# A mixture-of-experts block: experts placed by load, 12 in pairs of 64 slots and 52 in fours of 32 slots

## The chip, the cores and the metric

One core of a Trainium2 chip runs the whole block in one launch. The metric is the device time of that core in microseconds (us). Three runs of the kernel before took 1903.79, 1905.90 and 1906.02 us; their median is 1905.9 us.

## The reference

A transformer block on 512 tokens of width 1024 in float32: a differential attention, a state-space branch, their merge, and then a mixture of 64 experts. Only the last part is changed:

```python
# h2: 512 x 1024 tokens after the norm; each token goes to 2 of the 64 experts (1024 assignments)
g_sel  = argmax(h2 @ w_gr + b_gr)                 # one of 8 groups of 8 experts
top_i  = top_k((h2 @ w_er + b_er)[g_sel], 2)      # two experts inside the group
weight = softmax(group)[g_sel] * softmax(top_v)
# for each expert e, on its tokens x:
y = (silu(x @ w_gate[e]) * (x @ w_up[e])) @ w_down[e]    # 1024 -> 512 -> 1024
out[token] += weight * y
return rms_norm(x + out) * final_norm_w
```

How many tokens an expert gets is known only once the router has run on the chip. The reference has no limit on it.

## The kernel before

Ahead of the experts come the projections, attention, the state-space branch and the router, ordered by a planner (`Flow`), which places jobs by costs written in the code. The experts' part is written out by hand, in program order for each engine.

**Work of a pair.** The loop at L1702 takes 32 pairs of experts in the order of their numbers. An expert has 64 slots; the 128 slots of a pair fill the 128 columns of TensorE's array as two column tiles of 64. For a pair, `gate_up` (L1627) runs over 8 pieces k of the contraction: for each expert of the pair a gate matmul and an up matmul of 128x64 stationary activations against 128x512 float32 weights (each recorded as two matmul instructions, so 64 in all for a pair). `combine` (L1685) adds the outputs of the pair before to the tokens by 16 matmuls, which DVE adds to `x`. `hidden_t` (L1644) turns the hidden activations, `slots` (L1612) builds the matrix that scatters slots back to tokens, `down` (L1653) runs 4 pieces of the down projection (32 recorded matmuls), `weighted` (L1665) scales and splits the result. Every second pair, `onehot` (L1404) makes the 0/1 matrix that picks tokens for the next four experts by comparing their ranks in the table `rk1` with 1 to 64, and `gather` (L1601) applies it by 64 matmuls to give the activations `xt` of the next two pairs.

**Weights.** The expert weights are 64 x 6 MB, loaded by SP's DMA queue alone. A tile of 1 MB holds piece k of both experts of a pair; `tiles` (L1195) lists 12 of them per pair in the order of use. `issue` (L1203) starts one load; every fifteenth tile goes to two staging buffers in two halves. There is room for 15 tiles. `free` and `fill` (L1548, L1551), called by `done` (L1690) after every piece k, issue the next load as soon as its buffer is free. The first 15 tiles are loaded ahead of the experts' part, while the router still runs. The last tile is loaded in four parts (L1561).

**Experts with more than 64 tokens.** `overflow_tables` (L1565), run by DVE in the first pair, lists further rounds of 64 slots for them. Behind the pairs, a loop at L1741 runs as often as the table says, with weights whose address comes from a register. The first number of the table is read into a register of every engine (L1739). The last combination, the final norm and the stores follow (L1772 on). `keep_warm` (L298) issues matmuls whose result is not used.

Of the kernel before, what the change touches and what calls it, by code (L numbers as in the profile page):

```python
# [24 lines left out]
class Flow:  # L25
    """Orders the work of the engines: every job names an engine, its length and the jobs it needs."""
# [92 lines left out]
def block_kernel(ctx: ExitStack, tc: tile.TileContext, I, out):  # L119
# [158 lines left out]
    G.iota(iota1, pattern=[[1, 64]], base=1, channel_multiplier=0, allow_small_or_imprecise_dtypes=True)  # L278
    rev8 = cst([128, 8], "rev8")
# [864 lines left out]
    class Part:  # L1144
        """A row of the merged activations, cut into halves of the tokens; part 0 or 1 of the split."""
# [49 lines left out]
    tiles = []  # L1195
    for p in range(32):
        tiles += [("gu", p, k) for k in range(8)] + [("dn", p, k) for k in range(4)]
# [3 lines left out]
    NE = NB - 6 + NX  # L1201

    def issue():  # L1203
        n = nxt["i"]
        nxt["i"] += 1
        kind, p, k = tiles[n]
        src = I[kind][p, :, k]
        if n % NE == XS:
            t = [stage(), stage()]
        else:  # L1210
            b = (mt("ewx", [128, 2048], "ew") if n % NE == 0 else big("ew")).rearrange("p (e n) -> p e n", e=2)
            t = [b[:, 0], b[:, 1]]
        wt[kind, p, k] = t
        if n + 1 == len(tiles):
            return
        if n % NE == XS:
# [169 lines left out]
    def rtabs():  # L1386
        R["ovi"] = mt(None, [128, 64], "ovi", I32)
        R["base"] = mt(None, [128, 16], "base")
# [15 lines left out]
    def onehot(p, cs=range(NCH)):  # L1404
        if 0 in cs:
            R["P", p] = mt("P", [128, NCH, 4, E], "P", F32R)
        for c in cs:
            V.tensor_tensor(R["P", p][:, c], rk1[:, c, 4 * p:4 * p + 4].unsqueeze(2).to_broadcast([128, 4, E]),  # L1408
                            iota1[:, None, :].to_broadcast([128, 4, E]), op=OP.is_equal)
        return R["P", p].rearrange("p c e s -> p c (e s)")  # L1410
# [12 lines left out]
    def route(cl, prev):  # L1423
# [46 lines left out]
        def rk():  # L1470
            V.scalar_tensor_tensor(rk1[:, cs].rearrange("p c e -> p (c e)"), R["rps"][:, cl[0] * E:cl[-1] * E + E], 1.0,
                                   R["ab"][:, cs].rearrange("p c g e -> p (c g e)"), op0=OP.add, op1=OP.mult)
            R["P0"] = onehot(0, cl)
# [77 lines left out]
    def fill():  # L1551
# [3 lines left out]
        if nxt["i"] == len(tiles) and not nxt["end"]:  # L1555
            nxt["end"] = True
            kind, p, k = tiles[-1]
            for i in range(2):
                h = slice(i * 512, i * 512 + 512)
                for e in range(2):  # L1560
                    nc.sync.dma_start(wt[kind, p, k][e][:, h], I[kind][p, :, k, e, h])  # L1561

    fill()

    def overflow_tables():  # L1565
        ex = mt("y", [128, 1024], "ex")
        ext, pe, pf = (ex[:, i * E:i * E + E] for i in range(3))
        io, ef = ex[:, 256:272], ex[:, 320:384]
        V.tensor_scalar(ext, R["cnt"], 64.0, None, op0=OP.is_gt)
        for m in range(2, 8):  # L1570
            V.scalar_tensor_tensor(ext, R["cnt"], 64.0 * m, ext, op0=OP.is_gt, op1=OP.add)
        a, b = ext, pe
        for sft in (1, 2, 4, 8, 16, 32):
# [3 lines left out]
        V.tensor_scalar(io, iota1[:, :16], -1.0, None, op0=OP.add)  # L1577
        le = mt("y", [128, 16, E], "le")
        V.tensor_tensor(le, a[:, None, :].to_broadcast([128, 16, E]), io.unsqueeze(2).to_broadcast([128, 16, E]),
                        op=OP.is_le)  # L1580
        V.memset(ef, 0.0)
        V.tensor_copy(ef[:, 0:1], a[:, E - 1:E])
        V.tensor_reduce(ef[:, 1:17], le, axis=AX.X, op=OP.add)
        V.tensor_scalar(ef[:, 1:17], ef[:, 1:17], float(E - 1), None, op0=OP.min)
        V.tensor_scalar(ef[:, 17:33], ef[:, 1:17], 0.5, -0.25, op0=OP.mult, op1=OP.add)
        V.tensor_scalar(ef[:, 17:33], ef[:, 17:33], 12582912.0, None, op0=OP.add)
        V.tensor_scalar(ef[:, 17:33], ef[:, 17:33], 12582912.0, None, op0=OP.subtract)
        V.scalar_tensor_tensor(ef[:, 33:49], ef[:, 17:33], -2.0, ef[:, 1:17], op0=OP.mult, op1=OP.add)
        V.tensor_copy(R["ovi"], ef)
        V.tensor_tensor(le, le, ext[:, None, :].to_broadcast([128, 16, E]), op=OP.mult)  # L1590
        V.tensor_reduce(R["base"], le, axis=AX.X, op=OP.add)
        V.tensor_tensor(R["base"], iota1[:, :16], R["base"], op=OP.subtract)
        V.tensor_scalar(R["base"], R["base"], 64.0, None, op0=OP.mult)

# [17 lines left out]
    def slots(P, n, wcols):  # L1612
        w = 64 * n
        ps = side()
        for c in range(NCH):
            T.transpose(ps[:w, c * 128:c * 128 + 128], P[:, c].bitcast(F32), ident)
        pt = mt("pt", [128, 512], "pt", F32R)[:w]
        V.tensor_copy(pt, ps[:w])
        ws = side()
        for c in range(NCH):  # L1620
            T.matmul(ws[:w, :n], lhsT=P[:, c].bitcast(F32), rhs=wcols(c), start=(c == 0), stop=(c == 3))
        sl = pools["mp"].tile([128, 1], F32, name="sl", bufs=2)[:w]
        for e in range(n):
            V.tensor_scalar(sl[64 * e:64 * e + 64], ws[64 * e:64 * e + 64, e:e + 1], 0.5, None, op0=OP.mult)
        return pt, sl

    def gate_up(xt, n, gu, done, pre=lambda q: None):  # L1627
        w = 64 * n
# [9 lines left out]
        hh = mt("ta", [128, 512], "hh")[:w]  # L1638
        A.activation(hh, pg[:w], AF.Tanh, scale=0.5)  # L1639
        V.scalar_tensor_tensor(hh, hh, 1.0, pg[:w], op0=OP.add, op1=OP.mult)  # L1640
        V.tensor_tensor(hh, hh, pu[:w], op=OP.mult)
        return hh

    def hidden_t(hh, n):  # L1644
        w = 64 * n
        ps = side()
        for k in range(4):
            T.transpose(ps[:, k * w:k * w + w], hh[:, k * 128:k * 128 + 128], ident[:w, :w])
        ht = mt("ta", [128, 4, 128], "hT")[:, :, :w]
        A.activation(ht, ps[:, :4 * w].rearrange("p (k n) -> p k n", k=4), AF.Copy)  # L1650
        return ht

    def down(ht, n, dn, done):  # L1653
        w = 64 * n
        ps = [side(), side()]
        for k in range(4):
            for i in range(2):
                for e in range(n):
                    es_ = slice(64 * e, 64 * e + 64)
                    T.matmul(ps[i][es_], lhsT=ht[:, k, es_], rhs=dn(k)[e][:, i * 512:i * 512 + 512],  # L1660
                             start=(k == 0), stop=(k == 3), tile_position=(0, 64 * e))
# [3 lines left out]
    def weighted(ps, n, sl, yt=None):  # L1665
        w = 64 * n
        yh, yl = (yt or [mt("y", [128, 2, 512], n_, F32R) for n_ in ("yh", "yl")])
        yh, yl = yh[:w], yl[:w]
# [226 lines left out]
```

## Time and profile before

| | |
|---|---|
| median of 3 runs | 1905.9 us |
| span of the profiled execution | 1903.0 us |
| TensorE matmul busy | 1855.0 us (97%), 9551 matmuls |
| DVE busy | 893.9 us (47%) |
| ScalarE busy | 463.5 us (24%) |
| GpSimd busy | 315.9 us (17%) |
| DMA traffic | 475.24 MB, mean 250 GB/s |

The execution of the profile has a span of 1903.0 us, from its first to its last instruction; the median of the runs is 2.9 us longer. All rows are of this execution. In the page's 40 slices each slice is 47.6 us; the digits are tenths of a slice in which an engine was busy. A row of stages gives the stretch, then busy time and number of instructions of PE (matmuls), PEld (weight loads into the array), DVE, ACT and POOL, then the granted clock of TensorE (1.00 is full), the mean busy share of the 16 DMA engines, and what they moved. Rows of the order in time give start, duration, engine, line, operation, output<-input, shapes and count.

### The profile page before, as it was taken

Reading aid. Unit: us, or ns where it says so; the run is one execution under the profiler, and the core shown is the slowest. Engines: PE = TensorE matmul, PEld = TensorE weight load, DVE = VectorE, ACT = ScalarE, POOL = GpSimd, SP = SyncE. Lnnn points to the kernel's source line nnn. Section 1 sums busy time; section 2 is a strip of 40 time slices with the busy share of each in tenths; the row PEclk is TensorE's granted clock in tenths of the full one; section 3 lists DMA queues with packets and bytes.
Section 4 is the critical chain, followed back from the end, with each engine's and each line's share of the span. In section 5 each row is a group of like instructions: output and inputs, shape, how many; then the busy total and the mean of one; then the engine's idle time right before and its main releaser. Section 6 shows DMA issues by size and latency. Waiting matters only on the chain. (4 is left out here: it accounts for less than half of the span.)

```text
span 1903.0 us, 24077 instructions
## 1 busy us (share of the span) xinstructions
PE 1855.0 (97%) x9551; PEld 1208.8 (64%) x9551; DVE 893.9 (47%) x1659; ACT 463.5 (24%) x913; POOL 315.9 (17%) x330
## 2 busy tenths in 40 slices
PE   8999999999999999998999999999999999999996
PEld 6877788878787787885554555455545554555453
DVE  7687832587886945444432323232323232323234
ACT  5355530344443422121111111011101110111012
POOL 5243321253544442111000000000000000000001
PEclk9999999999999999998999999999999999999998
DMA  5311123212222222467899999999999999999991
GB/s 163 100 56 46 45 80 98 78 56 89 68 67 77 78 78 89 149 239 286 349 421 393 397 392 420 394 395 393 421 395 395 398 418 393 399 395 405 406 396 71
DMA packets 81042, 475.24 MB, mean 250 GB/s; under 512 B 10145, under 2 KB 10529, under 8 KB 34977
## 3 DMA queue, kind: packets, MB, share of 16 engines
q1 hardware_dynamic: 80928, 473.70, 64.1%
q8 instruction: 76, 1.25, 0.3%
q14 instruction: 38, 0.30, 0.0%
HBM read 471.56 MB, written 2.10 MB: 249 GB/s over the span
## 5 line engine op out<-in xcount | busy, mean ns | idle before, releaser
L1635 PE MATMUL g<-ew,xt 128*64 128x512 f32 x1896 | 418.7, 594 | 0.0
L243 PE MATMUL g<-hH,w 128*128 128x512 f32 x1024 | 344.6, 401 | 0.0
L1635 PEld LDWEIGHTS g<-ew,xt 128*64 128x64 f32 x1896 | 169.1, 137 | 236.3 <-issue 231.0
L243 PEld LDWEIGHTS g<-hH,w 128*128 128x128 f32 x1024 | 192.4, 188 | 43.1 <-issue 5.3
L1660 PE MATMUL s<-ew,hT 128*64 128x512 f32 x968 | 216.0, 595 | 0.7 <-ACT hT L1650 0.7
L1640 DVE SCALAR_TENSOR_TENSOR hh<-hh,g 128x512 f32<-128x512 f32 x32 | 22.0, 688 | 411.6 <-ACT hh L1639 411.6
L243 PE MATMUL g<-hL,w 128*128 128x512 f32 x512 | 199.9, 390 | 0.0
L1796 POOL TENSOR_TENSOR fst<-fst 128x1 f32<-128x1 f32 x4 | 1.2, 301 | 1020.6 <-ACT fo L1789 1020.6
L203 DVE TENSOR_TENSOR w<-stg,w 128x1024 fp32r<-128x1024 f32 x108 | 140.9, 1313 | 55.7 <-ACT w L200 32.2
L1683 DVE TENSOR_TENSOR x<-x,s 128x512 f32<-128x512 f32 x256 | 155.8, 681 | 8.3 <-PE s L1678 8.3
L1660 PEld LDWEIGHTS s<-ew,hT 128*64 128x64 f32 x968 | 66.7, 137 | 121.3 <-issue 119.9
L1671 DVE SCALAR_TENSOR_TENSOR yl<-s,sl,yh 128x512 fp32r<-128x512 f32 x64 | 48.0, 751 | 182.3 <-ACT yh L1670 180.8
L1418 PE MATMUL s<-P,h2H 128*128 128x256 f32 x512 | 125.2, 286 | 2.4 <-DVE P L1408 2.4
L1677 PE MATMUL s<-yh,pt 128*128 128x512 f32 x256 | 113.5, 443 | 11.9 <-DVE x L1683 9.7
L1419 PE MATMUL s<-P,h2L 128*128 128x256 f32 x512 | 122.7, 282 | 0.0
L1639 ACT ACTIVATE hh<-g 128x512 f32<-128x512 f32 x32 | 19.2, 599 | 412.4 <-PE g L1635 412.4
L198 POOL TENSOR_SCALAR w<-stg 128x1024 fp32r<-128x1024 f32 x60 | 69.0, 1150 | 264.3 <-DMA stg<-in_wu_dram 178.3
L243 PEld LDWEIGHTS g<-hL,w 128*128 128x128 f32 x512 | 96.4, 188 | 16.9
L1418 PEld LDWEIGHTS s<-P,h2H 128*128 128x128 f32 x512 | 96.9, 189 | 10.1 <-issue 7.4
L1678 PE MATMUL s<-yl,pt 128*128 128x512 f32 x256 | 100.9, 394 | 0.0
L1670 ACT ACTIVATE yh<-s,sl 128x512 fp32r<-128x512 f32 x64 | 43.9, 687 | 231.8 <-PE s L1660 219.9
L1419 PEld LDWEIGHTS s<-P,h2L 128*128 128x128 f32 x512 | 97.0, 190 | 0.0
(312 smaller groups left out, 2666.1 us busy)
## 6 DMA issues: line engine op xcount, KB each, us to landing
ew<-in_gu_dram SPq DMA_DIRECT2D x237, 1024.0 KB, 11.0
ew<-in_dn_dram SPq DMA_DIRECT2D x120, 1024.0 KB, 14.6
stg<-in_wu_dram SPq DMA_DIRECT2D x120, 512.0 KB, 3.6
stg<-in_gu_dram SPq DMA_DIRECT2D x38, 512.0 KB, 9.9
stg<-in_dn_dram SPq DMA_DIRECT2D x14, 512.0 KB, 14.3
xT<-in_xT_dram SPq DMA_DIRECT2D x4, 512.0 KB, 5.7
x<-in_xn_dram SPq DMA_DIRECT2D x2, 1024.0 KB, 9.9
out_dram<-fo SPq DMA_DIRECT2D x8, 256.0 KB, 2.1
```

Of the source, the lines that this page charges most:

```text
L198: G.tensor_scalar(c["h"], c["st"], 1.0, 0.0, op0=OP.mult, op1=OP.add)
L203: (G if i % 10 == 9 else V).tensor_tensor(c["lo"], c["st"], c["h"].bitcast(F32), op=OP.subtract)
L243: T.matmul(cell[b], lhsT=x, rhs=y, start=first and i == 0, stop=last and i == 2)
L1418: T.matmul(o, lhsT=h2(h2H, c)[:, d], rhs=P[:, c], start=(c == 0), stop=False)
L1419: T.matmul(o, lhsT=h2(h2L, c)[:, d], rhs=P[:, c], start=False, stop=(c == NCH - 1))
L1635: T.matmul(o[es_], lhsT=xt[:, k, es_], rhs=gu(k)[e][:, i * 512:i * 512 + 512], start=(k == 0), stop=(k == 7), tile_position=(0, 64 * e))
L1660: T.matmul(ps[i][es_], lhsT=ht[:, k, es_], rhs=dn(k)[e][:, i * 512:i * 512 + 512], start=(k == 0), stop=(k == 3), tile_position=(0, 64 * e))
L1670: A.activation(yh[:, i], ps[i][:w], AF.Copy, scale=sl[:, :1])
L1671: V.scalar_tensor_tensor(yl[:, i], ps[i][:w], sl[:, :1], yh[:, i].bitcast(F32), op0=OP.mult, op1=OP.subtract)
L1677: T.matmul(ps, lhsT=pt[:, c * 128:c * 128 + 128], rhs=yh[:, i], start=True, stop=False)
L1678: T.matmul(ps, lhsT=pt[:, c * 128:c * 128 + 128], rhs=yl[:, i], start=False, stop=True)
L1683: V.tensor_tensor(o, o, ps, op=OP.add)
```

## The change

The experts get places by their number of tokens, found on the chip. Experts 0 to 3 keep places 0 to 3 (their first weights are loaded before the counts exist); the others follow by falling count. Places 0 to 11 are 6 pairs with 64 slots for each, places 12 to 63 are 13 groups of four with 32 slots for each, as four column tiles of 32. Nineteen groups take the place of 32 pairs. A new `order_tables`, run in the first group, sorts the counts, permutes the rank and weight tables by matmuls, and leaves the list `perm` of expert numbers by place. From place 4 on, SP reads the expert's number from `perm` into a register and loads the weights from an address made with it. A tile of 1 MB now holds two pieces k of one expert, buffers are given back after every second k, and the last four tiles are loaded in twelve parts. Rounds for too full experts count from 64 slots in places 0 to 11 and from 32 in the others. The arrays of weights lie in memory by expert.

```diff
+    NS, NW = 4, 12
+    groups = ([list(range(i, i + 2)) for i in range(0, NW, 2)] + [list(range(i, i + 4)) for i in range(NW, 64, 4)])
     tiles = []
-    for p in range(32):
-        tiles += [("gu", p, k) for k in range(8)] + [("dn", p, k) for k in range(4)]
+    for g_ in groups:
+        tiles += [("gu", e, q) for q in range(4) for e in g_] + [("dn", e, q) for q in range(2) for e in g_]
...
+    def source(kind, e, q):
+        if e < NS:
+            return I[kind][e, :, 2 * q:2 * q + 2]
+        if e not in place:
+            place[e] = nc.values_load(R["perm"][0:1, e:e + 1], engines=[mybir.EngineType.SP], min_val=0, max_val=63,
+                                      skip_runtime_bounds_check_because=why)
+        return I[kind][bass.ds(place[e], 1), :, 2 * q:2 * q + 2].rearrange("o p k n -> (o p) k n")
...
+            for tl_ in tiles[-LASTN:]:
+                nc.sync.dma_start(wt[tl_][0], source(*tl_)[:, 0])
             for i in range(2):
                 h = slice(i * 512, i * 512 + 512)
-                for e in range(2):
-                    nc.sync.dma_start(wt[kind, p, k][e][:, h], I[kind][p, :, k, e, h])
+                for tl_ in tiles[-LASTN:]:
+                    nc.sync.dma_start(wt[tl_][1][:, h], source(*tl_)[:, 1, h])
...
+    def order_tables():
+        ox = mt("y", [128, 1024], "ox")
+        key, i64, w1, lt_ = (ox[:, i * E:i * E + E] for i in range(4))
+        bd = ox[:, 512:640]
+        kc, pc, cc_ = (ox[:, i:i + 1] for i in (640, 641, 642))
+        tT = mt("y", [128, 4, 128], "tT")
+        V.tensor_scalar(key, R["cnt"], 64.0, None, op0=OP.mult)
+        V.tensor_tensor(key, key, iota1, op=OP.subtract)
+        V.tensor_scalar(key[:, :NS], iota1[:, :NS], -1.0, 1.0e6, op0=OP.mult, op1=OP.add)
+        V.tensor_tensor(i64, ident[:, :E], ident[:, E:], op=OP.add)
+        V.tensor_tensor(w1, key, i64, op=OP.mult)
+        V.tensor_reduce(kc, w1, axis=AX.X, op=OP.add)
+        V.tensor_scalar(lt_, key, kc, None, op0=OP.is_gt)
+        V.tensor_reduce(pc, lt_, axis=AX.X, op=OP.add)
+        V.tensor_scalar(pc, pc, 1.0, None, op0=OP.add)
+        V.memset(bd, 0.0)
+        for i in range(2):
+            r = slice(64 * i, 64 * i + 64)
+            V.tensor_scalar(bd[r, 64 * i:64 * i + 64], iota1[r], pc[r], None, op0=OP.is_equal)
+        ps = side()
+        T.matmul(ps[:1, :E], lhsT=pidx[:E], rhs=bd[:E, :E], start=True, stop=True)
+        V.tensor_copy(R["perm"], ps[:1, :E])
+        V.tensor_tensor(w1, R["cnt"], i64, op=OP.mult)
+        V.tensor_reduce(cc_, w1, axis=AX.X, op=OP.add)
+        ps = side()
+        T.matmul(ps[:, :E], lhsT=cc_[:E].to_broadcast([E, 128]), rhs=bd[:E, :E], start=True, stop=True)
+        V.tensor_copy(R["cnt"], ps[:, :E])
+        ps = side()
+        for i in range(4):
+            T.transpose(ps[:, 128 * i:128 * i + 128], ptab[:, i], ident)
+        A.activation(tT, ps.rearrange("p (i n) -> p i n", i=4), AF.Copy)
+        ps = side()
+        for i in range(4):
+            T.matmul(ps[:, 128 * i:128 * i + 128], lhsT=tT[:, i], rhs=bd, start=True, stop=True)
+        A.activation(ptab, ps.rearrange("p (i n) -> p i n", i=4), AF.Copy)
...
     def overflow_tables():
...
+        V.tensor_scalar(cm[:, :NW], cm[:, :NW], 64.0, None, op0=OP.subtract)
+        V.tensor_scalar(cm[:, NW:], cm[:, NW:], 32.0, None, op0=OP.subtract)
...
+        for i in range(2):
+            m = slice(16 * i, 16 * i + 16)
+            V.tensor_tensor(le, a[:, None, :].to_broadcast([128, 16, E]),
+                            io[:, m].unsqueeze(2).to_broadcast([128, 16, E]), op=OP.is_le)
+            V.tensor_reduce(ef[:, 1 + 16 * i:17 + 16 * i], le, axis=AX.X, op=OP.add)
+            V.tensor_tensor(le, le, ext[:, None, :].to_broadcast([128, 16, E]), op=OP.mult)
+            V.tensor_reduce(bs[:, m], le, axis=AX.X, op=OP.add)
...
-    def gate_up(xt, n, gu, done, pre=lambda q: None):
-        w = 64 * n
+    def gate_up(xt, n, w, gu, done, pre=lambda q: None):
+        W = n * w
         for k in range(8):
             pre(k)
-            for e in range(n):
-                es_ = slice(64 * e, 64 * e + 64)
-                for i, o in enumerate((pg, pu)):
-                    T.matmul(o[es_], lhsT=xt[:, k, es_], rhs=gu(k)[e][:, i * 512:i * 512 + 512],
-                             start=(k == 0), stop=(k == 7), tile_position=(0, 64 * e))
+            for i, o in enumerate((pg, pu)):
+                for e in range(n):
+                    es_ = slice(w * e, w * e + w)
+                    T.matmul(o[es_], lhsT=xt[:, k, es_], rhs=gu(e, k)[:, i * 512:i * 512 + 512],
+                             start=(k == 0), stop=(k == 7), tile_position=(0, w * e))
             done(k)
...
-    for p in range(32):
+    for gi, g_ in enumerate(groups):
+        n = len(g_)
+        w = 128 // n
+        last = gi == NG - 1
+
+        def done(k, n=n):
+            if k % 2:
+                free(n)
+                fill()
...
-        if p == 0:
-            ps_ = pair_slots(P, 0)
-        if p == 0:
-            overflow_tables()
-        elif p < 31:
+        if gi == 0:
+            ps_ = group_slots(P, 0)
+            order_tables()
+        elif not last:
             combine(*pend)
-        if p == 31:
+        if last:
             keep_warm(8)
-        ht = hidden_t(hh, 2)
+        ht = hidden_t(hh, 128)
+        if gi == 0:
+            overflow_tables()
...
-    A["gu"] = c(gu.reshape(32, 2, 8, 128, 1024).transpose(0, 3, 2, 1, 4))
-    A["dn"] = c(w_expert_down[0].reshape(32, 2, 4, 128, 1024).transpose(0, 3, 2, 1, 4))
+    A["gu"] = c(gu.transpose(0, 2, 1, 3))
+    A["dn"] = c(w_expert_down[0].reshape(64, 4, 128, 1024).transpose(0, 2, 1, 3))
```

`slots`, `hidden_t`, `down`, `weighted`, `onehot` and the loop for too full experts take the width of a slot range (64 or 32) as an argument and otherwise do what they did.

## Rows read from the trace of the kernel before

**Rows 1.** The page: the span in 40 slices, DMA share and rate.

```profile
DMA  5311123212222222467899999999999999999991
GB/s 163 100 56 46 45 80 98 78 56 89 68 67 77 78 78 89 149 239 286 349 421 393 397 392 420 394 395 393 421 395 395 398 418 393 399 395 405 406 396 71
```

**Rows 2.** Stages: the first six pairs, the other 26, stretches inside them.

```profile
911.40:1068.70 157.30, 155.56 (x818) 83.98 (x816) 51.07 (x96) 19.92 (x32) 0.00 (x0) 1.00 0.96 393
1068.70:1858.60 789.90, 780.62 (x4005) 405.09 (x4001) 232.91 (x425) 94.32 (x150) 0.00 (x0) 1.00 0.98 401
...
960.00:1000.00 40.00, 39.28 (x204) 21.65 (x200) 16.07 (x29) 5.00 (x9) 0.00 (x0) 1.00 1.01 420
1460.00:1480.00 20.00, 19.58 (x94) 9.20 (x92) 9.92 (x19) 2.57 (x4) 0.00 (x0) 1.00 1.02 425
...
1318.00:1320.00 2.00, 2.00 (x12) 0.71 (x10) 0.00 (x0) 0.00 (x0) 0.00 (x0) 1.00 0.40 164
```

**Rows 3.** Waits from 911 to 1858 us: SP's queue, then PE's weight loads.

```profile
SPq L1220 <- PE s L1660: 444.5, 111, 15.8
SPq L1220 <- PE g L1635: 272.5, 216, 1.4
...
PEld g L1635 <- DMA ew<-in_gu_dram: 4.0, 17, 0.2
```

**Rows 4.** PE in order of time: gate_up of the second pair and of the last.

```profile
911.87 13.95 PE L1635 MATMUL g<-ew,xt 128*64 128x512 f32 x64
...
1855.47 7.09 PE L1635 MATMUL g<-ew,xt 128*64 128x512 f32 x32
```

**Rows 5.** PE in order of time: down, and gather's matmuls at two clocks.

```profile
904.95 7.09 PE L1660 MATMUL s<-ew,hT 128*64 128x512 f32 x32
...
877.25 0.41 PE L1418 MATMUL s<-P,h2H 128*128 128x256 f32 x1
877.46 0.41 PE L1419 MATMUL s<-P,h2L 128*128 128x256 f32 x1
...
881.39 0.28 PE L1418 MATMUL s<-P,h2H 128*128 128x256 f32 x1
881.51 0.28 PE L1419 MATMUL s<-P,h2L 128*128 128x256 f32 x1
```

**Rows 6.** First pair in order of time: transposes, their copy, the overflow tables.

```profile
903.64 0.60 PE L1616 MATMUL s<-ident,P 128*128 128x128 f32 x4
...
903.84 0.60 ACT L1650 ACTIVATE hT<-s 128x512 f32<-128x512 f32 x1 [2.26 <-PE s L1648]
903.95 0.20 DVE L1569 TENSOR_SCALAR ex<-cnt 128x64 f32<-128x64 f32 x1
...
914.36 0.17 DVE L1593 TENSOR_SCALAR base<-base 128x16 f32<-128x16 f32 x1
```

**Rows 7.** SP: a load's issue, a register load (count: ns min/median/max), a load's landing.

```profile
L1220 SPq DMA_DIRECT2D ew<-in_gu_dram x237: 327/328/436, 800.4 to 1836.5; - x119
...
L1739 SPq TENSOR_LOAD <-ovi x1: 463/463/463, 1853.1 to 1853.1; - x1
...
ew<-in_gu_dram SPq DMA_DIRECT2D x237, 1024.0 KB, 11.0
```

**Rows 8.** The end: the weights' last stretch, the last scaling, the last wait.

```profile
1858.00:1860.00 2.00, 2.00 (x12) 0.91 (x10) 0.00 (x0) 0.00 (x0) 0.00 (x0) 1.00 0.31 121
...
1883.42 1.49 ACT L1670 ACTIVATE yh<-s,sl 128x512 fp32r<-128x512 f32 x2 [6.42 <-PE s L1660]
...
1899.27 0.66 DVEq L1891
```

**Rows 9.** Stages around the router: the granted clock after gaps in PE's work.

```profile
870.00:875.00 5.00, 1.77 (x20) 1.66 (x20) 4.12 (x20) 0.23 (x1) 0.00 (x0) 0.79 0.13 56
875.00:880.00 5.00, 5.00 (x23) 3.97 (x22) 2.91 (x15) 0.86 (x3) 0.00 (x0) 0.53 0.00 0
880.00:885.00 5.00, 5.00 (x30) 2.59 (x26) 0.11 (x1) 0.38 (x1) 0.00 (x0) 1.00 0.55 200
```

More of the change, by code (lines that the diff above doesn't have):

```diff
@@ L1201, in block_kernel @@
     NE = NB - 6 + NX
+    LASTN = 4
+    place = {}
+    why = "counts of 1024 assignments"
+    def source(kind, e, q):
[5 more added lines that the diff above has]
+        return I[kind][bass.ds(place[e], 1), :, 2 * q:2 * q + 2].rearrange("o p k n -> (o p) k n")
     def issue():
@@ L1205, in issue @@
         nxt["i"] += 1
-        kind, p, k = tiles[n]
-        src = I[kind][p, :, k]
+        kind, e, q = tiles[n]
         if n % NE == XS:
@@ L1565, in overflow_tables @@
     def overflow_tables():
         ex = mt("y", [128, 1024], "ex")
[L1567 to L1571, printed above, removed]
+        ext, pe, pf, ef = (ex[:, i * E:i * E + E] for i in range(4))
+        io = ex[:, 320:352]
+        cm = R["cnt"]
+        V.tensor_scalar(cm[:, :NW], cm[:, :NW], 64.0, None, op0=OP.subtract)
@@ L1572, in overflow_tables @@
+        V.tensor_scalar(cm[:, NW:], cm[:, NW:], 32.0, None, op0=OP.subtract)
+        V.tensor_scalar(ext, cm, 0.0, None, op0=OP.is_gt)
+        for m in range(1, 8):
+            V.scalar_tensor_tensor(ext, cm, 64.0 * m, ext, op0=OP.is_gt, op1=OP.add)
         a, b = ext, pe
@@ L1732, in block_kernel @@
-        yps = down(ht, 2, lambda k: wt["dn", p, k], done)
-        pend = (pt, *weighted(yps, 2, sl))
+        o = 128 * (gi % 2)
+        hh = gate_up(xt[:, :, o:o + 128], n, w, wk("gu"), done, pre)
+        if gi == 0:
+            ps_ = group_slots(P, 0)
+            order_tables()
+        elif not last:
+            combine(*pend)
+        if last:
+            keep_warm(8)
+        ht = hidden_t(hh, 128)
+        if gi == 0:
+            overflow_tables()
+        pt, sl = ps_
+        if gi % 2 == 0:
+            if not last:
+                ps_ = group_slots(P, gi + 1)
+            if gi + 2 < NG:
+                es = sum(groups[gi + 2:gi + 4], [])
+                P = onehot(es)
+        elif not last:
+            m = P.shape[2]
+            xt = rows(m)
+            gather(P, m, xt)
+            ps_ = group_slots(P, gi + 1)
@@ L1735, in block_kernel @@
+        yps = down(ht, n, w, wk("dn"), done)
+        pend = (pt, *weighted(yps, 128, sl))
     keep_warm(4)
[L1738 to L1739 removed]
+    nov = nc.values_load(R["ovi"][0:1, 0:1], min_val=0, max_val=31, skip_runtime_bounds_check_because=why)
     ET = mybir.EngineType
     with tc.For_i(0, nov, 1) as m:
[L1742 to L1744 removed]
+        e, ed = (nc.values_load(R["ovi"][0:1, bass.ds(m + 1, 1)], engines=[en], min_val=0, max_val=E - 1,
+                                skip_runtime_bounds_check_because=why) for en in (ET.DVE, ET.SP))
+        ed = nc.values_load(R["perm"][0:1, bass.ds(ed, 1)], engines=[ET.SP], min_val=0, max_val=E - 1,
+                            skip_runtime_bounds_check_because=why)
@@ L1764, in block_kernel @@
         gather(P1, E, xo)
-        pt1, sl1 = slots(P1, 1, lambda c: cw1[:, c:c + 1])
-        hh = gate_up(xo, 1, lambda k: ow["gu", k], odd)
-        ht = hidden_t(hh, 1)
+        pt1, sl1 = slots(P1, 1, E, lambda c: cw1[:, c:c + 1])
+        hh = gate_up(xo, 1, E, lambda e, k: ow["gu", k], odd)
+        ht = hidden_t(hh, E)
         yo = big("yo", F32R).rearrange("p (t i n) -> p t i n", t=2, i=2)
         yo = [yo[:, 0], yo[:, 1]]
-        combine(pt1, *weighted(down(ht, 1, lambda k: ow["dn", k], odd), 1, sl1, yo))
+        combine(pt1, *weighted(down(ht, 1, E, lambda e, k: ow["dn", k], odd), E, sl1, yo))
     fl.t = {e: 0.0 for e in "PVAGQ"}
```

144 lines of the change are left out of this document (63 added, 81 removed).

## The prediction

> **What bounds the kernel now.** I read the slices of the page first: from slice 20 on (about 950 us) the weights move at 392 to 421 GB/s with the DMA engines busy for nine tenths or more, until the last slice [rows 1]. Then the stages: from the seventh pair to the end of the stream the share is 0.98 and the rate 401 GB/s, with PE busy for 780.62 of 789.90 us [rows 2]. So two resources are near their limit at once, and the waits tell which one sets the pace. SP waits for matmuls of the pairs to give buffers back, 444.5 us for those of down and 272.5 us for those of gate_up, while PE's weight loads wait for weights for 4.0 us in all [rows 3]. PE is the bound. One pair takes (1855.47 - 911.87) / 30 = 31.45 us [rows 4]. The stream shows its own limit where it never runs dry: 420 GB/s over 40 us, and 425 in the best 20 us; between such stretches it falls to 164, where PE has no buffer to give back [rows 2]. A pair's 12 tiles of 1.049 MB, 12.58 MB, would take 29.96 us at 420. So the stream is 1.5 us per pair behind PE, no more: this is all that a faster PE can win from it.
>
> **The change, part by part.**
>
> *Fours.* A four needs 64 x 2 + 32 x 2 = 192 recorded matmuls of gate_up and down where a pair needs 96. In pairs, with two column tiles, 64 take 13.95 us and 32 take 7.09 us, 0.22 us each [rows 4, 5]; with four tiles side by side it would be 0.11 us. The bounds: 0.11 us each (21 us a four), and 0.22 us, nothing gained (42 us). That PE can start matmuls 0.12 us apart is shown by gather's [rows 5], so I take about 0.11. The rest of a pair's period, 31.45 - 21.0 = 10.4 us (combine, gather, slots, transposes, gaps), is per group and stays. PE so needs 31.5 to 52.7 us per four. The stream needs 24 x 1.049 MB / 420 GB/s = 59.9 us per four. At both ends PE is faster than the stream: from the first four on, the stream is the bound, whatever the overlap.
>
> *Pairs.* Places 0 to 11 stay 6 pairs at PE's pace, 31.45 us each. Freeing two tiles after every second k is later by at most one k, 13.95 / 8 = 1.7 us, with a store of 15 tiles; landing takes 11.0 us [rows 7]; PE doesn't see it. I cost it at 0 (bounds 0 and 1.7 x 6 = 10 us).
>
> *The stream in the fours.* From 1068.7 us to its end at 1858.6 us it moves 789.9 x 401 = 316.7 MB [rows 2]. At 420 GB/s that takes 754 us, 36 us less; at 425, the best, 745 us; at 401, if the dips are its own, 790 us. I take 420, as the longer stretch shows. By the Trainium skill, "DMA: Bandwidth & Descriptors", Specifications, HBM gives a core about 358 GB/s; the same bytes would take an estimated 885 us and a faster PE would bring nothing. The trace disagrees, with 401 GB/s over 789.9 us, and this enters no sum.
>
> *Order tables.* In group 0 they stand between gate_up and hidden_t. DVE's chain to `bd` is 12 small operations of some 0.2 us [rows 6], 2.5 us; then two small matmuls with copies, about 1.2 us; four transposes at 0.6 us for four, a copy of 0.60 us, four matmuls and a second copy of the same sizes [rows 6], 2.4 us; hops between engines about 1 us. Sum 7 us. PE waits for all of it, since slots, hidden_t and down are queued behind it, and down's matmuls are what frees the next buffers. The pairs that follow run at PE's pace, so this lands on the path: +7 us. Bounds: 0, if the loads still under way cover it, and 12 us. DVE's overflow tables (903.95 to 914.5 us, [rows 6]) get a second pass, some 5 us more, and start later; the scaling of group 0 and the one-hot of groups 2 and 3 are queued behind them on DVE, but PE meets their results only after the next gate_up, 14 us later. Cost 0.
>
> *Register loads on SP.* 60 loads at 0.46 us and 0.33 us for each issue [rows 7]; with address arithmetic, for which no row exists, I take 1 us per tile; SP is quick enough below 1.049 MB / 420 GB/s = 2.5 us. Bounds: 0.33 + 0.46 / 6 = 0.4 us, free, and 2.5 us, also free. The first register load waits for `perm`; queued behind it on SP is tile 24, while 0 to 23 have fixed addresses, and its buffer comes free only in down, after `perm` anyway. Cost 0. What it hides behind are up to 11 tiles in flight, 27 us; the stretch of a group in which nothing is freed is about 17 us.
>
> *The counts.* With the reference's inputs the fullest expert has 39 tokens and, in place order, the fullest from place 12 on has 21: no round for too full experts runs, before or after.
>
> *The end.* The profiled stream ends at 1858.6 us, 44 us ahead of the end, because a whole store is still to be worked off. With PE waiting for it, only the last matmuls follow (1.5 us with the landing), then what runs before too from the last scaling to the end: 1903.0 - 1883.4 = 19.6 us [rows 8]. Together 21.1 us. Bounds 19.6 and 26 us, for a low clock.
>
> **Sum:** 1068.7 + 7 + 754 + 21.1 = 1850.8 us as a span; the median stands 2.9 us above the profiled span, so 1853.7, rounded **1854 us**, 2.7% less than 1905.9. Most of PE's gain, 13 groups x 28 us, turns into PE's waiting for weights.
>
> **The rivals.**
>
> *The clock.* When PE waits for four tiles (10 us) and works for 3.5 us, its clock may fall. Around the router, with PE busy for 1.77 of 5 us, the granted clock went to 0.79 and then 0.53, towards the lower level of 1.2 GHz, and was 1.00 (2.4 GHz) again after 5 us of steady work [rows 9]; gather's matmuls then stood 0.21 us apart rather than 0.12 [rows 5]. A four all at the low level is at most 2 x 31.45 = 62.9 us against the stream's 59.9: 13 x 3 = 39 us more, **1893 us**. Against it: such a PE is never idle, and steady work brought the clock back. The Trainium skill, "TensorE: Matmul & The Clock Gate", section "HAM oscillation", describes this very loop of waits for DMA and a cold array; I expect the trace to show it in gate_up, hidden behind the stream. Chance 0.13 that it costs most of the 39 us.
>
> *The stream cannot do better than 401.* Then 1068.7 + 7 + 790 + 21.1 + 2.9 = **1890 us**. Addresses in registers or another stride in memory could do that too. For it: the share is 0.98 already. Against it: 420 over 40 us. Chance 0.12.
>
> *Column tiles of 32 do not run side by side (slower).* Before, 26 pairs took 62.9 us per four. With the 7 us of the tables the change loses once a four takes 62.9 - 7 / 13 = 62.4 us, that is (62.4 - 10.4) / 192 = 0.27 us per recorded matmul; one tile at a time, 0.43 us, gives 92 us a four and 1905.9 + 7 + 13 x 29.6 = **2298 us**. For it: no row shows four tiles. Against it: two tiles run at 0.22 us. Chance 0.06.
>
> *It doesn't do what it says:* places or counts off, so that a round for full experts runs behind the groups. Its 6 MB take 15 us and its work, in series, at least a pair's 31 us: about 46 us on top, **1900 us**. Chance 0.03.
>
> **How the numbers follow.** The forecast has 0.66. Its own range is 1836 us (no cost of the tables and 425 GB/s, with some of the end's bound) to 1868 us (tables 12 us, the end 26 us, some starvation). To leave out no more than two in ten, the range reaches up to the clock and to 401 GB/s: **1836 to 1893 us**. About 0.2%, 4 us, is what a measurement here can tell from no change. Faster by more than that: the forecast, the two rivals near 1890 and most of the last, 0.90; within it 0.03; slower 0.07.
>
> **What would show it.** Right: PE's weight loads wait for weights for hundreds of us; the DMA share is 1.01 without dips from some 1076 us to some 1830 us; the end follows about 21 us behind the stream; gate_up's matmuls in fours stand closer than 0.22 us; SP waits for matmuls far less. Wrong: dips in the stream within the fours with SP waiting for matmuls (PE late: clock or overlap), or with SP itself busy (registers); a rate under 410 at full share (memory); a stretch ahead of down in group 0 much longer than 7 us; any load of weights in the loop behind the groups.

## The result, and the profile after

The changed kernel takes **1857.85 us** (median of 4 runs, 1856.82 to 1860.44) against 1904.92 us in the same comparison: ratio 0.9757, 95% interval 0.9743 to 0.9771, that is 47.1 us or 2.5% less. The forecast was 1854 us. The profiled execution took 1860.44 us, with a span of 1858.6 us.

The page's slices of the kernel after, 46.5 us each: PE's busy share, the granted clock, the DMA share and rate.

```profile
PE   8999999999999999998899987868768776787675
...
PEclk8999999999999999998899998899899989999998
DMA  5311122222221223356699999999999999999995
GB/s 157 101 57 53 51 76 83 91 69 68 69 80 59 78 61 98 91 215 267 238 389 405 419 414 421 420 420 420 421 420 421 420 421 421 420 420 420 421 420 231
```

Where [rows 1] had 392 to 421 GB/s, the rate is now 420 or 421 in every slice from the 25th to the last but one. PE has gaps, 60 to 90% busy in a slice, and its clock falls below full there. The bound has moved from PE to the stream of weights.

The stages (columns as in [rows 2]): the order tables, the pairs behind group 0, the fours up to 1832 us, 20 us inside a four, and two stretches of the stream's end.

```profile
900.00:920.00 20.00, 15.16 (x68) 9.69 (x66) 12.80 (x49) 2.39 (x4) 0.00 (x0) 0.66 0.48 186
923.90:1080.90 157.00, 156.82 (x838) 79.95 (x838) 52.16 (x102) 20.81 (x34) 0.00 (x0) 1.00 0.99 402
1080.90:1832.00 751.10, 569.36 (x3274) 208.24 (x3266) 122.04 (x240) 46.04 (x75) 0.00 (x0) 0.91 1.01 419
1180.00:1200.00 20.00, 15.04 (x65) 3.04 (x64) 0.00 (x0) 0.00 (x0) 0.00 (x0) 0.74 1.02 419
1830.00:1832.00 2.00, 2.00 (x16) 0.64 (x8) 0.00 (x0) 0.00 (x0) 0.00 (x0) 1.00 0.87 298
1836.00:1838.00 2.00, 2.00 (x8) 0.44 (x8) 0.75 (x1) 0.69 (x1) 0.00 (x0) 1.00 0.05 19
```

In the pairs PE is busy for 156.82 of 157.00 us, as before. In the fours it is busy for 569 of 751 us while the DMA engines have no gap at all (share 1.01).

The waits from 911 to 1858 us (us in total, times, longest), SP's queue and PE, to be read against [rows 3]:

```profile
PEld g L1701 <- DMA ew<-in_gu_dram: 284.9, 152, 3.6
...
PE g L1701 <- DMA ew<-in_gu_dram: 159.6, 112, 2.7
...
SPq L1238 <- DMA ew<-in_gu_dram: 300.5, 155, 3.0
SPq L1238 <- DMA ew<-in_dn_dram: 135.0, 76, 2.4
SPq L1238 <- PE s L1724: 95.5, 24, 17.8
SPq L1238 <- PE g L1701: 50.8, 46, 2.4
```

PE's weight loads waited for weights for 4.0 us in all; now it is 284.9 us at gate_up alone. SP's waits for matmuls, 717 us before, are down to 146; what it waits for most are landings of earlier loads: it is held by the stream itself and no longer by PE.

The order tables in group 0, in order of time (start, duration, engine, line, operation, count, and the idle time before it with what ended it):

```profile
904.14 0.20 DVE L1595 TENSOR_SCALAR ox<-cnt 128x64 f32<-128x64 f32 x1
...
906.65 0.37 PE L1609 MATMUL s<-ox,pidx 64*1 64x64 f32 x2 [3.28 <-DVE ox L1607]
...
908.45 1.11 PE L1618 MATMUL s<-ident,ptab 128*128 128x128 f32 x4
...
910.31 2.07 PE L1622 MATMUL s<-ox,tT 128*128 128x128 f32 x8 [0.75 <-ACT tT L1619]
912.18 1.06 PE L1713 MATMUL s<-ident,hh 128*128 128x128 f32 x4
...
915.52 8.55 PE L1724 MATMUL s<-ew,hT 128*64 128x512 f32 x32
```

The granted clock in two stretches of it, PE's idle time and hidden_t with the slots:

```profile
904.00:906.60 2.60, 0.00 (x0) 0.00 (x0) 2.31 (x12) 0.00 (x0) 0.00 (x0) 0.66 0.99 321
...
912.20:915.50 3.30, 3.30 (x17) 3.30 (x15) 2.70 (x15) 1.20 (x2) 0.00 (x0) 0.50 0.00 0
```

PE is idle for 3.28 us while DVE works out the order, and then the four transposes take 1.11 us, where four took 0.60 before [rows 6]. The granted clock of the whole stretch (900 to 920 us) is 0.66: it falls in PE's idle time, is 0.50, the level of 1.2 GHz, from 906.6 to 918 us, and is 1.00 again from 920 us. Down starts at 915.52 instead of 904.95 [rows 5] and takes 8.55 us instead of 7.09.

The down step of a four, with its weights there:

```profile
1291.06 7.07 PE L1724 MATMUL s<-ew,hT 128*32 128x512 f32 x64
```

That is 64 matmuls in 7.07 us where a pair's 32 took 7.09 [rows 5]: 0.11 us each, side by side in four column tiles.

### The profile page after: what moved, and what is told of

It reads as the page before. It is cut to its first block, busy times and chain, and to the rows that moved or that the text cites. A ratio compares the mean times of both kernels' runs of the same rounds, so it can differ in the third digit from the quotient of the medians.

```text
span 1858.6 us, 22998 instructions
## 1 busy us (share of the span) xinstructions
PE 1636.6 (88%) x8767; PEld 1004.8 (54%) x8767; DVE 785.3 (42%) x1487; ACT 416.3 (22%) x839; POOL 316.9 (17%) x331
## 5 line engine op out<-in xcount | busy, mean ns | idle before, releaser
L1701 PE MATMUL g<-ew,xt 128*32 128x512 f32 (+1 forms) x1888 | 418.0, 696 | 159.8 <-DMA ew<-in_gu_dram 159.6
L1701 PEld LDWEIGHTS g<-ew,xt 128*32 128x32 f32 (+1 forms) x1888 | 96.7, 128 | 452.4 <-DMA ew<-in_gu_dram 284.6
L1724 PE MATMUL s<-ew,hT 128*32 128x512 f32 (+1 forms) x976 | 161.8, 614 | 19.3 <-DMA ew<-in_dn_dram 18.6
L1746 DVE TENSOR_TENSOR x<-x,s 128x512 f32<-128x512 f32 x152 | 92.4, 679 | 22.9 <-PE s L1741 22.9
L846 DVE SCALAR_TENSOR_TENSOR xb<-u,cw,xb 128x511 f32<-128x511 f32 (+2 forms) x96 | 81.7, 862 | 23.4 <-ACT xb L842 21.7
L1701 PE MATMUL g<-stg,xt 128*32 128x512 f32 (+1 forms) x160 | 88.3, 692 | 2.1 <-DMA stg<-in_gu_dram 1.8
L243 PE MATMUL g<-w,hH 128*128 128x512 f32 x256 | 84.3, 410 | 0.0
L1440 PE MATMUL s<-P,h2H 128*128 128x256 f32 (+1 forms) x320 | 78.5, 288 | 2.3 <-DVE P L1429 2.3
L243 PE MATMUL g<-sH,w 128*128 128x512 f32 x256 | 80.2, 394 | 0.0
L1441 PE MATMUL s<-P,h2L 128*128 128x256 f32 (+1 forms) x320 | 76.7, 282 | 0.0
```

What stands on the lines that cost most here:

```text
L243: T.matmul(cell[b], lhsT=x, rhs=y, start=first and i == 0, stop=last and i == 2)
L846: V.scalar_tensor_tensor(x()[:, 3 - k:], t["u"][:, :n], w[:, k:k + 1], x()[:, 3 - k:], op0=OP.mult, op1=OP.add)
L1440: T.matmul(o, lhsT=h2(h2H, c)[:, d], rhs=P[:, c], start=(c == 0), stop=False)
L1441: T.matmul(o, lhsT=h2(h2L, c)[:, d], rhs=P[:, c], start=False, stop=(c == NCH - 1))
L1701: T.matmul(o[es_], lhsT=xt[:, k, es_], rhs=gu(e, k)[:, i * 512:i * 512 + 512], start=(k == 0), stop=(k == 7), tile_position=(0, w * e))
L1724: T.matmul(ps[i][es_], lhsT=ht[:, k, es_], rhs=dn(e, k)[:, i * 512:i * 512 + 512], start=(k == 0), stop=(k == 3), tile_position=(0, w * e))
```

## The experiments

Lines of a diff with "-" are those of the changed kernel, unless another is named. All medians are set against the kernel before on the same chip, whose own medians there lie between 1904.6 and 1906.1 us.

**1. Pairs alone.** All 32 pairs, everything else as changed: order tables, addresses from registers, tiles by expert.

```diff
-    NS, NW = 4, 12
+    NS, NW = 4, 64
...
-    LASTN = 4
+    LASTN = 2
...
-        V.tensor_scalar(cm[:, NW:], cm[:, NW:], 32.0, None, op0=OP.subtract)
```

> All 64 experts as 32 pairs with 64 slots (NW = 64), everything else as changed: tables sorted on the chip, addresses from registers, tiles of one expert, the new order of matmuls. If the gain comes from the fours alone and the tables cost their 12 us: PE is the bound again at 31.4 us a pair, and the time is 1905 + 12 = 1917 us (1910 to 1922). If register addresses, the new tiles or the order of the matmuls bring part of the gain, it is below 1900. If register loads hold SP up, it is above 1925 with dips in the stream while SP is busy.

Measured: 1892.92 us (1892.37 to 1893.52), ratio 0.9934 (0.9917 to 0.9951), 24 us less than expected, and faster than the kernel before though it has the order tables on top. Its pairs take 34.2 and 27.0 us in turn (odd and even ones, with and without gather). Before, they took 35.1 and 27.8. So something outside the fours makes a pair 0.87 us shorter, on the mean of 30. Before, `combine` runs like this:

```profile
1401.24 0.50 PE L1677 MATMUL s<-yh,pt 128*128 128x512 f32 x1
1401.37 0.60 ACT L1639 ACTIVATE hh<-g 128x512 f32<-128x512 f32 x1 [13.11 <-PE g L1635]
...
1403.40 4.27 DVE L1683 TENSOR_TENSOR x<-x,s 128x512 f32<-128x512 f32 x7
...
1404.14 0.50 PE L1677 MATMUL s<-yh,pt 128*128 128x512 f32 x1 [0.31 <-DVE x L1683]
...
1405.93 0.66 PE L1648 MATMUL s<-ident,hh 128*128 128x128 f32 x4
```

ACT's activation needs the gate matmuls of both experts, and behind the second expert's last gate matmul only one up matmul of gate_up is left. So it starts 0.13 us after combine's first matmul. DVE's additions to `x` are queued behind DVE's two steps on the activation's result and start 2.2 us into combine, and PE's last matmuls wait for them. The changed `gate_up` has gate and up as the outer loop and the experts inside, so that two up matmuls follow the last gate matmul. Experiment 2 tests this alone.

**2. The loop order alone**, in the kernel before ("-" is the kernel before here):

```diff
-            for e in range(n):
-                es_ = slice(64 * e, 64 * e + 64)
-                for i, o in enumerate((pg, pu)):
+            for i, o in enumerate((pg, pu)):
+                for e in range(n):
+                    es_ = slice(64 * e, 64 * e + 64)
```

> The kernel before, with one thing of the change: in gate_up the loop over gate and up is outside that over the two experts. The gate sums are then complete 0.8 us earlier, and the chain ScalarE, DVE to the hidden activations with them, so that DVE's additions of combine start earlier and PE waits less for them. If this explains the 0.84 us by which pairs are shorter in the run with 32 pairs, the time is 1905 - 31 x 0.84 = 1879 us (1876 to 1884), still at PE's pace (30.6 against the stream's 30.0 us a pair). If the shorter pairs come from the tiles of one expert, from freeing two at a time or from the addresses, it stays at 1905.

Measured: 1877.45 us (1876.82 to 1878.60), ratio 0.9856 (0.9840 to 0.9872); pairs of 34.2 and 27.0 us. The same place in order of time:

```profile
1386.11 0.60 ACT L1639 ACTIVATE hh<-g 128x512 f32<-128x512 f32 x1 [12.24 <-PE g L1635]
...
1386.79 0.50 PE L1677 MATMUL s<-yh,pt 128*128 128x512 f32 x1
...
1388.14 4.87 DVE L1683 TENSOR_TENSOR x<-x,s 128x512 f32<-128x512 f32 x8
...
1390.67 0.65 PE L1648 MATMUL s<-ident,hh 128*128 128x128 f32 x4
```

The activation now starts 0.68 us ahead of combine, DVE's additions 1.35 us into it, no matmul is shown waiting, and combine takes 3.88 us instead of 4.69. That is nearly all of the 0.87 us: gate_up itself hardly changes, with 13.83 us instead of 13.88 from its first matmul to combine's. Three swapped lines so bring 27.5 us by themselves. With them in, the fours have less left to win: 1877.45 plus 12 us for the order tables is 1889, and the change is at 1858, so the fours are worth some 31 us. (Experiment 1 is 3.5 us above this 1889; it has an idle time at its end which experiment 10 shows.) And most of the 31 us (29 between the two profiled spans) are won at the end. Here the last load of weights lands at 1833.4 us, with 41.9 us of work behind it; in the changed kernel it lands at 1837.9 us, after the 12 us of the tables, with 20.6 us behind it. The stream so ends some 7 us sooner by itself, and 21 us go because no full store of weights is left to work off.

**3 and 4. Do four column tiles overlap, and how far?** Each group of matmuls in fours is issued twice, or three times (the outputs count each product of the fours twice, or three times):

```diff
             for i, o in enumerate((pg, pu)):
-                for e in range(n):
...
+                m = 2 if n == 4 else 1
+                for r in range(m):
+                    for e in range(n):
...
```

and the same in `down`.

> In the fours every gate, up and down matmul is issued twice (the products are counted twice in the output). PE then needs some 10.4 + 2 x 21 = 52.4 us for a four, the stream 59.9. If the stream is the bound in the fours: 1858 us, plus at most 4 us at the end, where the last matmuls have nothing to hide behind. If PE's pace still counted there, it would be up to 13 x 21 = 273 us longer.

> In the fours every gate, up and down matmul is issued three times (the products are counted three times in the output). PE then needs some 10.4 + 3 x 21 = 73.4 us for a four, more than the stream's 59.9. If the bound is whichever of the two is longer, the fours take 13 x 73.4 = 954 us and the time is some 2055 us (2030 to 2075), with PE waiting for weights almost nowhere. If the four column tiles do not run fully side by side, it is longer still: at 30 us for a four's matmuls, 100 us a four, some 2400 us.

Measured: 1869.40 us (1865.78 to 1871.57) with two, 2024.65 us (one run) with three. The stretch from 1180 to 1780 us with two, then with three:

```profile
1180.00:1780.00 600.00, 548.05 (x4454) 213.71 (x4448) 96.04 (x190) 36.78 (x60) 0.00 (x0) 0.99 1.02 420
```

```profile
1180.00:1780.00 600.00, 599.00 (x5360) 234.39 (x5352) 84.21 (x167) 33.69 (x54) 0.00 (x0) 1.00 0.88 349
```

With twice the matmuls the stream still runs at 420 GB/s. With three times PE is the bound and a four takes 68.0 and 75.0 us in turn, 71.5 on the mean where 73.4 were expected, so that the time is 5 us below the expected range. A group's other work is (34.2 + 27.0) / 2 - 21.0 = 9.6 us, so a recorded matmul costs (71.5 - 9.6) / 576 = 0.107 us, half of the 0.22 of two tiles [rows 4]: the overlap is complete. By the Trainium skill, "TensorEngine Tiling (Array Packing)", Theoretical Speedup, tiles of at most 32 give up to four times; the trace agrees on the step from two tiles to four, with 0.22 and 0.107 us. PE's own need is 9.6 + 20.6 = 30 us a four, half of what the stream takes. The version with two has a profiled span 8.8 us longer than the change's (1867.4 us). That is more than the 4 us that the expectation allowed. All of it lies behind the stream: 4.4 us up to the last scaling, as the last down is issued twice, and 4.4 behind it, for which see experiment 10.

**5. What the order tables cost.** Experts stay in the order of their numbers, all addresses are fixed, and `order_tables` isn't called (a token beyond the 32nd of an expert in a four is left out):

```diff
-        if e < NS:
+        if True:
             return I[kind][e, :, 2 * q:2 * q + 2]
...
-            order_tables()
...
-        V.tensor_copy(ef[:, 0:1], a[:, E - 1:E])
```

> The sort is left out: experts keep their numbers as places, all addresses are fixed, the sorting tables are not built, and tokens beyond 32 in places from 12 on are left out. The rest is as changed. If the sort costs just the delay ahead of down in group 0 (12 us) and register loads cost nothing: 1858 - 12 = 1846 us (1843 to 1849). If the register loads or the computed addresses cost something in the stream, it is lower than 1840. If the delay is made up later, it stays at 1858.

Measured: 1845.58 us (1843.52 to 1846.42), ratio 0.9683 (0.9667 to 0.9699), as expected: 12.3 us less than the change. Group 0 takes 32.0 us instead of 44.2, and the fours keep their 60 us. So the tables cost 12 us, nearly all of it in group 0, and the register loads with their addresses cost nothing that can be measured.

**6. Half the weights.** Only the first of a tile's two pieces is loaded in the experts' part and used for both:

```diff
-            for i in range(2):
-                nc.sync.dma_start(t[i], src[:, i])
+            nc.sync.dma_start(t[0], src[:, 0])
         else:
-            nc.sync.dma_start(b, src)
+            nc.sync.dma_start(b[:, 0], src[:, 0])
```

> Only the first of the two pieces in a tile of weights is loaded, and it serves for both (half of the weights' traffic is left out, the work of PE stays). If a four costs PE some 9.7 + 20.6 = 30.3 us, as the run with three times the matmuls says, the fours take 13 x 30.3 = 394 us in place of 755, and the time is some 1858 - 361 = 1497 us (1485 to 1510). If the four column tiles overlap only by two, a four takes 51 us and the time is some 1770 us.

Measured: 1533.43 us (one run), 36 us above the expectation for a full overlap and far below that for none. With half the bytes the fours are not PE's alone yet:

```profile
1080.00:1500.00 420.00, 411.71 (x3208) 186.01 (x3202) 120.04 (x237) 44.32 (x72) 0.00 (x0) 1.00 0.95 371
```

PE is 98% busy and the DMA engines 95%: both are near their limit, as 12.58 MB a four need 30 us at 420 GB/s, just PE's own 30 us. This is no clean number for PE, but it shows that the stream set the time in the fours: 324 us go when half of it is gone.

**7. The order tables beside down.** The permutation matmuls are put between the steps of group 0's `down`, the tables for too full experts into group 1, and group 0's one-hot matrix behind its down:

```diff
-            order_tables()
+            mid = order_tables()
...
-    def down(ht, n, w, dn, done):
+    def down(ht, n, w, dn, done, mid=lambda k: None):
...
+            mid(k)
```

> Order tables beside other work: DVE's chain runs while PE goes on with hidden_t and slots, PE's part stands between the pieces of down in group 0 (after the first and the third), the overflow tables move into group 1. Group 0 then takes some 37 us in place of 44, of which two changes of the tile form and the table's own matmuls are 5. If this delay lands on the end one to one, as the run without the sort says: 1858 - 7 = 1851 us (1848 to 1853). If the stream makes it up, 1858.

Measured: 1850.93 us (1849.71 to 1852.04), ratio 0.9715 (0.9701 to 0.9728). Group 0 takes 35.5 us instead of 44.2, and 6.9 of the tables' 12 us are back. PE now has hardly any idle time there, and its clock stays up, where it was 0.66 in the change. The same transposes and the matmuls behind them take 0.66 and 1.16 us (second block), where they took 1.11 and 2.07:

```profile
903.00:925.00 22.00, 21.56 (x109) 8.46 (x110) 6.67 (x24) 2.71 (x5) 0.00 (x0) 1.00 0.89 334
```

```profile
906.67 0.66 PE L1620 MATMUL s<-ident,ptab 128*128 128x128 f32 x4 [0.29 <-DVE pt L1688]
...
910.84 1.16 PE L1625 MATMUL s<-ox,tT 128*128 128x128 f32 x8
```

**8. Pairs among the fours,** on top of 7. The pairs are PE's, the fours are the stream's; in turn, the store of 15 tiles lets one cover the other:

```diff
+    groups = groups[:2] + groups[6:8] + groups[2:4] + groups[8:10] + groups[4:6] + groups[10:]
```

> As the run before, and the pairs of places 4 to 11 are no longer in a row: two pairs, two fours, two pairs, two fours, two pairs, the other nine fours. In a row PE needs 30.6 us for a pair where the stream needs 30.0, and the stream waits; between fours PE has time in hand. Four pairs at 0.6 us, and the stream is full from some 985 us on rather than 1080: it moves 402 GB/s there in place of 420, so 95 us x 0.043 = 4 us. Expected 1847 us (1844 to 1850). If the stream's rate in the pairs is its own limit, 1851.

Measured: 1848.01 us (1847.58 to 1849.15), ratio 0.9702 (0.9689 to 0.9716), the fastest that leaves nothing out (only experiment 5 is below it), 10 us below the change. Where the run before moved 409 GB/s in the pairs from 985 to 1070 us, the stream is now full:

```profile
985.00:1080.00 95.00, 78.09 (x438) 32.44 (x432) 20.08 (x36) 8.92 (x14) 0.00 (x0) 0.96 1.02 420
```

**9. Fewer parts at the end,** on top of 8 ("-" is that version). The last parts of the stream move at 290 to 300 GB/s, as the stages above show; is it their size?

```diff
-            for i in range(2):
-                h = slice(i * 512, i * 512 + 512)
-                for tl_ in tiles[-LASTN:]:
-                    nc.sync.dma_start(wt[tl_][1][:, h], source(*tl_)[:, 1, h])
+            for tl_ in tiles[-LASTN:]:
+                nc.sync.dma_start(wt[tl_][1], source(*tl_)[:, 1])
```

> The spread version with the last four tiles loaded in 8 parts of 512 KB, where it had 4 of 512 KB and 8 of 256 KB. In the changed kernel the last parts of the stream moved at some 290 GB/s rather than 420. If the size of the parts is what slows them, the last 4.2 MB come about 3 us sooner, and TensorE has 4 more small steps behind the last landing, some 1 us: 1846 us (1844 to 1848), against 1848.0 for the spread version. If they are slow because the queue runs empty behind the last load, nothing is gained and the later landing of whole parts costs 0 to 2 us: 1848 to 1850 us.

Measured: 1848.42 us (1847.56 to 1849.28), no gain. The parts of 512 KB still move at less than 350 GB/s:

```profile
1814.00:1816.00 2.00, 1.31 (x12) 0.54 (x14) 0.00 (x0) 0.60 (x1) 0.00 (x0) 1.00 0.99 348
...
1818.00:1820.00 2.00, 2.00 (x15) 0.69 (x8) 0.00 (x0) 0.00 (x0) 0.00 (x0) 1.00 0.81 315
```

That the queue runs empty fits this; what slows the last parts was not settled further.

**10 and 11. Does the low clock cost time?** Matmuls whose result is not used, 32 at three places of gate_up in every four, then 24:

```diff
             pre(k)
+            if n == 4 and k in (2, 4, 6):
+                keep_warm(32)
```

> The changed kernel with 32 matmuls of 128x128 whose result is not used put in front of pieces 2, 4 and 6 of gate_up in every four, so that TensorE has less idle time while it waits for weights. If the low clock in the fours (0.91 on the mean, down to 0.74 in some stretches) is hidden behind the weight stream, as I think: the granted clock in the fours rises to 0.97 or more, the stream stays at 419 to 421 GB/s and the time stays at 1858 us (1855 to 1862). If the low clock costs time in the fours, the same clock brings 10 to 39 us back: 1819 to 1848 us. If the unused matmuls get in the way of the real ones, over 1862 us.

Measured: 1866.38 us (1862.61 to 1867.23), ratio 0.9791 (0.9776 to 0.9806), 8.5 us above the change. By the number alone that is the third case of the expectation; the trace puts it elsewhere. In the fours the clock is up and the stream runs at the rate it had:

```profile
1180.00:1780.00 600.00, 565.41 (x4500) 365.38 (x4492) 95.38 (x190) 36.80 (x60) 0.00 (x0) 0.99 1.01 420
```

The profiled spans differ by 6.3 us (1864.9 against 1858.6). The last scaling starts 2.0 us later (1841.03 against 1839.05 us), as the last load of weights lands 2.0 us later; why is open, and with 24 matmuls it does not. The other 4.3 us lie behind the scaling, first of all ahead of the last combination:

```profile
1840.93 1.16 PE L303 MATMUL s<-ident 128*128 128x128 f32 x8
...
1846.82 0.80 PE L1740 MATMUL s<-yh,pt 128*128 128x512 f32 x1 [4.74 <-issue]
1847.42 0.63 PE L1741 MATMUL s<-yl,pt 128*128 128x512 f32 x1
```

The DMA queues between 1844 and 1849 us (transfers, MB, share):

```profile
q8 instruction: 1, 0.02, 1.5%
```

PE is idle for 4.74 us "issue", that is, waiting for nothing that the profile shows, where it was 1.81 us in the changed kernel; after it the matmuls are 0.43 us apart instead of 0.23. In the changed kernel one transfer of instructions, of 0.02 MB, begins in its gap, at 1841.4 us, 0.5 us before PE goes on. Here two begin in the gap, at 1843.2 us and at 1846.4 us (the one shown), the second 0.4 us before PE goes on. The version with two matmuls for one, which happens to have the same number of PE instructions (11263), has the same gap (4.83 us) with two transfers in it. So has experiment 1, with pairs alone and 9567 PE instructions:

```profile
1874.15 0.79 PE L1739 MATMUL s<-yh,pt 128*128 128x512 f32 x1 [4.83 <-issue]
```

The version with three matmuls, which has more instructions (13759), has neither the second transfer nor the gap (1.78 us).

> The version with unused matmuls in the fours, with 24 instead of 32 at each of the three places (13 x 3 x 8 x 2 = 624 recorded matmuls fewer). With 32 the stream kept its 420 GB/s and ended within 2 us of the changed kernel's, but the last combination began 4.7 us after the last matmuls instead of 1.8 and ran at the low clock, which made up some 6 of the 8.5 us. If that gap depends on how the instructions happen to lie and not on the work in the fours, it goes with this other count: 1858 to 1862 us, the granted clock in the fours still over 0.96. If the work in the fours itself delays the end, it stays: 1864 to 1867 us.

Measured: 1860.94 us (1856.24 to 1862.33), ratio 0.9764 (0.9747 to 0.9781). With another count the gap is 1.81 us again, without a second transfer, and the stage of the fours reads

```profile
1080.90:1832.00 751.10, 695.02 (x5142) 410.47 (x5130) 121.36 (x239) 45.55 (x74) 0.00 (x0) 0.97 1.01 419
```

So PE at 0.97 of its clock, and 93% busy, has the same stream and no shorter time than at 0.91 and 76%. The low clock in the fours costs nothing that can be measured, and the gap does not go with the amount of work. That it goes with how the instructions lie, and that PE waited for code there, is what the second transfer suggests; it is not shown.

## Why the prediction was right, and where it was off

The forecast was 1853.7 us, the measurement 1857.85. By its steps:

*What bounds it.* Right. PE was the bound and the stream 1.5 us per pair behind it; now the stream is the bound, and experiments 3 and 6 show both sides: doubled matmuls leave the stream at 420 GB/s, halved weights take 324 us off.

*Fours.* Right at the lower bound: 0.107 us against about 0.11. The four takes (1778.6 - 1117.6) / 11 = 60.1 us by gate_up's starts, forecast 59.9. Where PE's need lies between 31.5 and 52.7 us did not matter, as argued; the measured one is 30, just below.

*The stream.* Right: 755 us from the first four to its end at about 1836 us, forecast 754 at 420 GB/s. The dips to 164 GB/s before were PE's doing.

*Order tables.* Forecast 7 us (0 to 12), measured 12: experiment 5 prices them, group 0's 44.2 us against 32.0 show it. One of the prediction's own signs of being wrong, a stretch ahead of down much longer than 7 us, is there: 10.57 us. DVE's chain was sized well (2.5 us from 904.14 us to the first matmul's start, forecast 2.5). What was left out is that PE's idle time there brings its clock down, so that what follows costs more, up to nearly double: 1.11 us for the transposes where 0.60 were taken, 1.06 instead of 0.66 for hidden_t's, and 8.55 instead of 7.09 for down. One term was too small by itself: the four matmuls behind the transposes are recorded as eight and take 1.16 us at full clock (experiment 7), 2.07 here, where 0.60 were taken. Of the 12.03 us, 9.04 lie ahead of hidden_t, 1.53 in hidden_t and the slots, and 1.46 in down; the last two, 3.0 us, are operations that ran before too, at the low clock. Experiment 7, with PE kept busy, has the clock at 1.00 there. [Rows 9] had shown the like around the router; the prediction used it for the fours alone.

*Pairs.* Costed at 0, and the swapped loop order not looked at: it makes each pair 0.87 us shorter (experiment 2). That is the step that the prediction missed altogether. It did little harm here, because only 5 of the pairs behind group 0 remain at PE's pace (4.2 us), and, by luck, because it met an error of the other sign: pairs take 35.1 and 27.8 us in turn, and the five behind the first begin and end with a long one, so that the seventh began at 1072.8 us, not at 1068.7 as the mean gave. The fours begin at 1072.8 + 12.0 - 4.2 = 1080.6 us, forecast 1075.7.

*Register loads.* Costed at 0; experiment 5 agrees, as fixed addresses leave the fours at 60 us. The 60 loads took 0.27 us each in the median, where the prediction had 0.46; the 1 us per tile that it took for issue and address was not measured.

*The end.* Forecast 21.1 us behind the stream, measured 1858.6 - 1835.6 = 23.0. From the last scaling on it is 19.5 us, as forecast (19.6); ahead of it there are 3.4 us, where the forecast had 1.5. The last twelve parts move at some 290 to 300 GB/s, and down's last steps wait for them; the forecast had them at the full rate.

*Sum.* 4.9 us for the later start, 1.0 for the stream, 1.9 for the end: 7.8 above the forecast span of 1850.8, which gives 1858.6. The median stands 0.75 us below this span, not 2.9 above, because the profiled execution was the slowest of the four; this takes 3.65 back by luck and leaves 1857.85.

*The rivals.* The clock: it does fall, to 0.74 in the stretch shown, and by experiment 11 that is hidden. The Trainium skill, "TensorE: Matmul & The Clock Gate", HAM oscillation, describes such a loop; the trace agrees on the fall, and the price that the rival gave it, up to 39 us, is not there. A stream of 401 at most: refuted by 419 over 751 us. For the stream the prediction cited the Trainium skill's 358 GB/s for a core. The Trainium skill, "HBM Reference", Specifications (TRN2), adds that a core streaming alone reaches about 425, and the trace agrees with that, with 419 here. Tiles not side by side: refuted by experiment 4. Places or counts off: the last load of weights is issued at 1832.7 us, for the last group, and none behind the groups.

## What to carry to other kernels

When two resources stand within a few per cent of each other, the gain of making one faster ends at the other: a four needs 30 us of TensorE and 60 of the stream, so of the some 31 us that TensorE saves in each of 13 fours (two pairs need 61) only some 31 us in all reach the end, and some two thirds of these come from work that no longer stands behind the last load. Serial work on a side engine cost more than its sum here, because the idle TensorE came back at the low clock: put it beside other matmuls (6.9 of 12 us came back that way). And price the reordered lines of a diff too: which result is complete first decides when the next engine starts, and three lines alone bring 27.5 us, where the whole change brings 47.1.

## What was not expected of the hardware

- An order of matmuls that changes no amount of work made a pair 0.87 us shorter, 27.5 us over 32 pairs, through ACT's and DVE's queues.
- Three kernels, two with 2496 more PE instructions than the change and one with 800 more, had an idle time of 4.7 to 4.8 us instead of 1.8 ahead of the last combination, each with two instruction transfers of 0.02 MB begun in it instead of one; with 1872 or 4992 more it was not there. With the low clock after it, that is some 4 us which do not come from the work that was added in the fours.
- The last loads of the stream, of 512 KB and of 256 KB, moved at 290 to 350 GB/s, where the loads of 1 MB ahead of them moved at 420.
